# Full block masks, a softmax sink that is added on VectorE, and S5 output matrices written once to HBM and read back in long runs

## The chip, the cores and the metric

The kernel runs on one core of one Trainium2 chip, in one launch. The metric is the device time in microseconds (us). Three runs of the kernel before took 2862.04, 2859.88 and 2861.97 us; the median is 2861.97.

In the profile PE is TensorE's matmuls, PEld its weight loads, DVE VectorE, ACT ScalarE, POOL GpSimd, and SP the sync engine, which issues most DMAs. A name such as L1287 is a line of the kernel.

## The reference

Two transformer blocks over 512 positions of width 1024. The first has two layers, each with a full attention, a windowed attention with a sink, a Fourier mix, a spatial gate and a gated merge. The second has a Mamba-2 and a diff-attention layer, then one with S5 and MLA, each followed by a feed-forward network. Three places matter here. The windowed attention puts one more column, the learned sink of the head, into the softmax and drops it again:

```python
s_sink = jnp.broadcast_to(sink_f[None, :, :, None, None], s_loc.shape[:-1] + (1,))
p = jax.nn.softmax(jnp.concatenate([s_ctx, s_loc, s_sink], axis=-1), axis=-1).astype(vv.dtype)
return (jnp.einsum('bkgqn,bnkd->bqkgd', p[..., :nc], vc)
        + jnp.einsum('bkgqj,bjkd->bqkgd', p[..., nc:nc + 3 * Q_BLOCK], vv))
```

The diff attention and MLA mask their scores by chunks of 64 positions, `jax.nn.softmax(jnp.where(mask, s.astype(F32), -jnp.inf), axis=-1)`: a query sees all keys up to the end of its own chunk. In a diagonal block of 128 x 128 this masks the keys 64 to 127 for the queries 0 to 63. The S5 group is a linear state-space recurrence for 32 groups of 16 channels; the kernel works it in blocks of 8 steps, so that the output is a product of the input with shifted copies of one kernel matrix for each group, plus a product of the block's start state.

## The kernel before

Positions stand in tiles of 128 on the partitions, features in columns, or the other way round. A product in full precision is three matmuls of high and low parts (`mm3`, L237 to L239). Weights come by `wload` (L218): a 1 MB load on SP (L225) into one of two raw buffers, a cast on ScalarE (L232) and a subtraction on VectorE and GpSimd (L233). The tile framework's scheduler sets the order of instructions on each engine by dependencies and priority; only the order of the program is written out.

**Windowed attention, `attn1` (L1035).** Items are pairs of a query block and a head. `scores` multiplies queries with the high and low part of the keys (L1075, L1076), adds 128x128 block masks as a matmul with the bf16 identity as weights (L1078, `mb_id`), and writes the sink to column 768 by a matmul of one row of ones with the head's sink (L1081). There are 40 of these: 24 in layer 0 (two streams) and 16 in layer 1. A reduce takes the negated maximum (L1083), an exponential follows with a running sum (L1087). One item later come the transposes (L1097), two to three items later the values (L1111) and the division by the sum (L1122). Two score buffers in PSUM, `at`, alternate.

**Block masks of the second block, `causal64` (L1285).** The diagonal block gets its mask by a matmul with one row: weights that are 1 for the first 64 queries, times a row that is a large negative number for the last 64 keys. Diff attention calls it 64 times (tiles `dat`, after L1414 and L1415), MLA 32 times (tiles `mat`, after L2182).

**S5.** `s5_coef` (L1854) is a generator that runs beside the merge of layer 1. It works out, for four sets of 8 groups, the input matrices (`d_bm`), output matrices (`d_ca`) and kernel rows (`d_kk`, L1971) and stores each in HBM. In `odd` (L1980) the recurrence runs on VectorE in 63 steps (L2072 to L2078) beside MLA. Then comes the output. Eight DMAs read shifted windows of `d_kk` (L2237), each to 16 partitions, in pieces of 128 numbers:

```python
tt_ = self.tl(yp, [P, 32, P], F32, "s5T")
kk = self.d_kk
for k in range(8):
    nc.sync.dma_start(tt_[16 * k:16 * k + 16], kk[:, :, 16 * k:16 * k + 128])
```

For each half `pb` two loads bring `d_ca` (L2242, tiles `s5ca`), and groups of matmuls with s5T (L2250) and s5ca (L2252) follow. A few matmuls of the projection of the layer's other output (`residual`, `side`) are woven in.

Of the kernel before, what the change touches and what calls it, by code (L numbers as in the profile page):

```python
# [9 lines left out]
F32 = mybir.dt.float32  # L10
F32R = mybir.dt.float32r
BF16 = mybir.dt.bfloat16
I32 = mybir.dt.int32
AF = mybir.ActivationFunctionType
ALU = mybir.AluOpType
AX = mybir.AxisListType
PSUM = bass.MemoryType.PSUM
P = 128
# [78 lines left out]
class Kern:  # L97
# [75 lines left out]
    def setup1(self):  # L173

        nc, I = self.nc, self.I
        nc.gpsimd.dma_start(self.cst[:, P:], I["cst"][:, P:CST_KEEP])
        mk = self.mk = self.tl(self.vp, [P, 2, P], F32, "mk")
        nc.gpsimd.dma_start(mk, I["cst"][:, CST_KEEP:].rearrange("p (a b) -> p a b", a=2))
        self.sink = self.tl(self.cp, [1, 8], F32, "sink")
        nc.gpsimd.dma_start(self.sink, I["sink_d"].rearrange("a b -> (a b)").unsqueeze(0))  # L180
        for gi in (1, 2):
            self.vec_load(gi, nc.gpsimd)

    def setup_cols(self):
        for gi in (1, 2):
            self.vec_cols(gi)
        mb = self.tl(self.cp, [P, 3, P], BF16, "mb")
        self.mb_id, self.mb_prev, self.mb_next = mb[:, 0, :], mb[:, 1, :], mb[:, 2, :]
        self.G.tensor_copy(mb[:, 0, :], self.ident)
        self.G.tensor_copy(mb[:, 1:3, :], self.mk)  # L190

    def vec_load(self, gi, q):
        vr = self.vr[gi] = self.tl(self.vp, [P, P], F32, f"vr{gi}")
# [841 lines left out]
    def attn1(self, l, hds, tr, Y, full, ap, at, fills):  # L1035


        nc, V, S, G, T = self.nc, self.V, self.S, self.G, self.T
        items = [(br, i, pair, qi, j) for br in range(2) for pair in range(2) for i in ((0, 1) if full else (0,))
                 for qi in range((4, 2)[i]) for j in range(2)]  # L1040
        st = {}

        def scores(m):
            br, i, pair, qi, j = items[m]
            for f in fills:
                first, last, rate, gen, done = f
                if m >= last and (done is None or not done()):
                    for _ in gen:
                        if done is not None and done():
                            break  # L1050
                elif m >= first:
                    for _ in range(rate):
                        next(gen, None)
            tq, kh, kl = tr[br, pair]

            if i == 1:
                segs, c0 = [(512, 512, 256, ())], 512
            elif br == 0:
                segs, c0 = [(0, 0, 512, ()), (512, 512, 256, ())], 0
            else:  # L1060
                b0, b1 = max(qi - 1, 0), min(qi + 2, 4)
                nl = (b1 - b0) * P
                c0 = 512 - nl
                mk = []
                if b0 < qi:
                    mk.append((c0, self.mb_prev))
                if b1 > qi + 1:
                    mk.append((512 - P, self.mb_next))
                segs = [(c0, b0 * P, nl, mk), (512, 512, 256, ())]
            c1 = 768 + (1 if br == 1 else 0)  # L1070
            kts = [(pc + u * P, kc // P + u) for pc, kc, w, _ in segs for u in range(w // P)]
            sc = self.tl(at, [P, 1024], F32, "at")
            q0 = qi * P + (512 if i == 1 else 0)
            for pc, kc, w, mk in segs:
                T.matmul(sc[:, pc:pc + w], tq[j][:, q0:q0 + P], kh[:, kc:kc + w], start=True, stop=False)  # L1075
                T.matmul(sc[:, pc:pc + w], tq[j][:, q0:q0 + P], kl[:, kc:kc + w], start=False, stop=not mk)  # L1076
                for x, (mc, mask) in enumerate(mk):
                    T.matmul(sc[:, mc:mc + P], self.mb_id, mask, start=False, stop=x == len(mk) - 1)  # L1078
            if br == 1:
                h = l * 4 + 2 * pair + j  # L1080
                T.matmul(sc[:, 768:769], self.ones[0:1, :], self.sink[0:1, h:h + 1], start=True, stop=True)  # L1081
            mx = self.tl(self.sm, [P, 1], F32, "mx", bufs=8)
            V.tensor_reduce(mx, sc[:, c0:c1], AX.X, ALU.max, negate=True)  # L1083
            e = self.tl(ap, [P, 772], F32, "e", bufs=3)
            if qi + j == 0:
                st["sum"] = self.tl(self.sm, [P, 4, 2], F32, "sme", bufs=3)
            S.activation(e[:, c0:c1], sc[:, c0:c1], AF.Exp, bias=mx, accum_out=st["sum"][:, qi, j:j + 1])  # L1087
            st[m] = (e, kts, st["sum"])

        def transposes(m):  # L1090
            e, kts, sums = st[m]
            pt = self.tl(ap, [P, 6, P], F32, "pt", bufs=4)
            for g0 in range(0, len(kts), 4):
                grp = kts[g0:g0 + 4]
                tp = self.tl(self.tp, [P, 512], F32, "tp")
                for x, (pc, _) in enumerate(grp):
                    T.transpose(tp[:, x * P:(x + 1) * P], e[:, pc:pc + P], self.ident)  # L1097
                n = len(grp)
                (V.tensor_copy if g0 else S.copy)(pt[:, g0:g0 + n, :].rearrange("p a b -> p (a b)"), tp[:, :n * P])
            st[m] = (pt, kts, sums)  # L1100

        def values(m):
            br, i, pair, qi, _ = items[m]
            if qi == 0:
                st["po"] = self.mt()
            po = st["po"]
            _, kts, sums = st[m]
            v = hds[br][2]
            for x, (_, kt) in enumerate(kts):
                for j in range(2):  # L1110
                    T.matmul(po[64 * j:64 * j + 64, qi * P:(qi + 1) * P], v[:, kt, pair * 64:pair * 64 + 64],  # L1111
                             st[m - 1 + j][0][:, x, :], start=(x == 0), stop=(x == len(kts) - 1))
            nq = (4, 2)[i]
            if qi == nq - 1:
                self.normalised(Y(br, pair)[i][0], po, sums, nq, ap, "pt", 4)

        self.pipeline(len(items), ((scores, 0, 1), (transposes, 2, 1), (values, 3, 2)))
# [36 lines left out]
class Kern2(Kern):  # L1154
# [129 lines left out]

    def causal64(self, sc, qi):  # L1285

        self.T.matmul(sc[:, qi * P:(qi + 1) * P], self.mrow[0:1, 0, :], self.mrow[0:1, 1, :], start=False, stop=True)  # L1287

    def setup2_load(self):
        V = self.V  # L1290
        self.mrow = self.tl(self.cp, [1, 2, P], BF16, "mrow")
        V.memset(self.mrow, 0.0)
        V.memset(self.mrow[:, 0, 0:64], 1.0)
        V.memset(self.mrow[:, 1, 64:128], NEG)
        self.pos = self.tl(self.cp, [P, 4], I32, "pos")
        self.nc.gpsimd.dma_start(self.pos, self.I["positions_2"][0].rearrange("(t p) -> p t", p=P))

# [526 lines left out]
class Kern3(Kern2):  # L1824
# [22 lines left out]
    def s5_alloc(self):  # L1847
        dp = self.ctx.enter_context(self.tc.tile_pool(name="s5d", bufs=1, space=bass.MemoryType.DRAM))
        self.d_bm = [self.tl(dp, [P, 4, 2, P], F32, f"dbm{b}") for b in range(4)]
        self.d_ca = [self.tl(dp, [P, 2, 8, 64], F32, f"dca{b}") for b in range(4)]  # L1850
        self.d_kk = self.tl(dp, [16, 32, 15 * 16], F32, "dkk")
        self.a8 = self.tl(self.cp, [P, 2, 2, 16], F32, "a8")

    def s5_coef(self, pool):  # L1854
# [55 lines left out]
        for ub in range(4):  # L1910
# [61 lines left out]
            if ub == 0:  # L1972
                zt = self.tl(pool, [16, 112], F32, "s5z")
                V.memset(zt, 0.0)
                for b in range(4):
                    nc.sync.dma_start(self.d_kk[:, 8 * b:8 * b + 8, 0:112], zt.unsqueeze(1).to_broadcast([16, 8, 112]))
            yield


    def odd(self):  # L1980
# [250 lines left out]

        ys = ExitStack()
        yp = self.pool(ys, "s5y")
        tt_ = self.tl(yp, [P, 32, P], F32, "s5T")
        kk = self.d_kk
        for k in range(8):
            nc.sync.dma_start(tt_[16 * k:16 * k + 16], kk[:, :, 16 * k:16 * k + 128])  # L2237
        Y = self.tl(yp, [P, 2, 8, 8, 16], F32, "s5Y")
        for pb in range(2):
            ca = [self.tl(yp, [P, 2, 8, 4, 16], F32, f"s5ca{g2}") for g2 in range(2)]  # L2240
            for g2 in range(2):
                nc.sync.dma_start(ca[g2].rearrange("p r k u h -> p r k (u h)"), self.d_ca[2 * g2 + pb])  # L2242
            pss = [self.mt() for _ in range(2)]
            for u in range(4):
                for ri in range(3):
                    for o, g2 in ((0, 0), (1, 1), (0, 1), (1, 0)):
                        g = g2 * 16 + o * 8 + pb * 4 + u
                        dst = pss[o][64 * g2:64 * g2 + 64, u * P:(u + 1) * P]
                        if ri == 0:
                            T.matmul(dst, U[:, g, :], tt_[:, g, :], start=True, stop=False)  # L2250
                        else:
                            T.matmul(dst, xp3[64 * o:64 * o + 64, ri - 1, g2 * 8 + pb * 4 + u, :],  # L2252
                                     ca[g2][64 * o:64 * o + 64, ri - 1, :, u, :], start=False, stop=(ri == 2))
# [93 lines left out]
```

## Time and profile before

| what | value |
| --- | --- |
| median of three runs | 2861.97 us |
| the profiled execution's own time | 2858.03 us |
| its span | 2856.1 us |
| mean granted TensorE clock | 0.987 |
| TensorE busy | 2758.6 us, 97% |
| TensorE weight loads | 2287.8 us, 80% |
| VectorE busy | 1418.5 us, 50% |
| ScalarE busy | 1000.1 us, 35% |
| GpSimd busy | 897.6 us, 31% |
| HBM read, written | 231.54 MB, 6.78 MB |

The span runs from the first to the last instruction; the execution's own time is a little longer. Busy times of matmuls overlap, since they are pipelined: a record's duration is longer than the distance to the next start, and so the price of a matmul is read from starts. A weight load can lie beside the matmul before it.

### The profile page before, as it was taken

The page shows a single profiled execution, that of the slowest core. Times are in us where ns is not written, and L with a number is a line of the kernel's source. Part 1 is how long each engine was busy: PE and PEld are TensorE (multiplying, and loading weights), DVE is VectorE, ACT ScalarE, POOL GpSimd, SP SyncE. Part 2 cuts the span into 40 slices and gives each one's busy share as a digit, 9 for nine tenths or more (in the row PEclk, how much of TensorE's full clock was granted, in tenths as well). Part 3 has the DMA queues.
Part 4 walks back from the last instruction along what each step waited for, and adds up shares of the span by engine and source line. Part 5 has one row for each costly group of instructions (what it writes and reads, how often), then busy time and mean ns, then how long its engine had stood idle before and what let it go on. Part 6 is the DMA issues. An engine that isn't in the chain of part 4 may idle for free.

```text
span 2856.1 us, 39868 instructions
## 1 busy us (share of the span) xinstructions
PE 2758.6 (97%) x15976; PEld 2287.8 (80%) x15976; DVE 1418.5 (50%) x2786; ACT 1000.1 (35%) x1796; POOL 897.6 (31%) x684
## 2 busy tenths in 40 slices
PE   7999999999998999999999989999999997999998
PEld 4976888888897888888887767788888865788887
DVE  5634411113255556344667786655532384665532
ACT  3335422222343542333455333323322252432222
POOL 4400343232233134334221233533323220343332
PEclk9999999999999999999999999999999998999999
DMA  7235122121322114332322221222323204233232
GB/s 243 66 101 184 58 63 74 56 60 63 104 76 79 42 46 133 110 106 78 97 64 78 53 89 45 74 89 89 103 96 96 85 31 82 82 103 103 89 100 85
DMA packets 221165, 248.23 MB, mean 87 GB/s; under 512 B 14191, under 2 KB 205268, under 8 KB 219956
## 3 DMA queue, kind: packets, MB, share of 16 engines
q1 hardware_dynamic: 218788, 240.76, 27.3%
q0 software_dynamic: 2192, 4.93, 0.9%
q8 instruction: 125, 2.05, 0.3%
q14 instruction: 60, 0.49, 0.1%
HBM read 231.54 MB, written 6.78 MB: 83 GB/s over the span
## 4 chain that ended last, share of the span: by engine, by line
PE 42%; DVE 4%; issue 4%; DMA 2%; ACT 1%; POOL 1%; SPq 0%; ACTq 0%; POOLq 0%; DVEq 0%
PE ex L238 7%; PE ex L237 7%; PE ex L239 7%; PE mm L237 5%; PE mm L238 5%; PE mm L239 5%; DVE xs L1516 1%; PE mat L2182 1%; DMA dk<-dk 1%; PE sg L1680 1%; DMA s5T<-dkk 1%; DVE wlo L233 0%; PE mpo L2212 0%; DMA dcol<-in_ev_d_skip 0%; PE tp L2199 0%
## 5 line engine op out<-in xcount | busy, mean ns | idle before, releaser
L233 POOL TENSOR_TENSOR wlo<-wraw,whi 128x1024 fp32r<-128x1024 f32 (+3 forms) x180 | 440.4, 2447 | 888.4 <-ACT whi L232 882.2
L232 ACT CAST whi<-wraw 128x1024 fp32r<-128x1024 f32 (+2 forms) x360 | 351.6, 1006 | 600.1 <-issue 208.8
L233 DVE TENSOR_TENSOR wlo<-wraw,whi 128x1024 fp32r<-128x1024 f32 (+2 forms) x180 | 238.3, 1324 | 383.1 <-ACT whi L232 382.5
L239 PE MATMUL ex<-hhi,wlo 128*128 128x512 f32 x1044 | 408.5, 391 | 7.0 <-DVE wlo L233 7.0
L237 PE MATMUL ex<-hhi,whi 128*128 128x512 f32 x1044 | 410.0, 393 | 0.6 <-ACT whi L232 0.6
L238 PE MATMUL ex<-hlo,whi 128*128 128x512 f32 x1044 | 408.0, 391 | 0.0
L237 PE MATMUL mm<-hhi,whi 128*128 128x512 f32 x708 | 282.2, 399 | 2.4 <-ACT whi L232 2.3
L238 PE MATMUL mm<-hlo,whi 128*128 128x512 f32 x708 | 279.1, 394 | 3.1 <-DVE hlo L329 2.8
L239 PE MATMUL mm<-hhi,wlo 128*128 128x512 f32 x708 | 279.0, 394 | 2.6 <-DVE wlo L233 2.5
L239 PEld LDWEIGHTS ex<-hhi,wlo 128*128 128x128 f32 x1044 | 196.5, 188 | 50.0 <-DVE wlo L233 8.6
L237 PEld LDWEIGHTS ex<-hhi,whi 128*128 128x128 f32 x1044 | 196.6, 188 | 41.8 <-ACT whi L232 1.4
L238 PEld LDWEIGHTS ex<-hlo,whi 128*128 128x128 f32 x1044 | 196.7, 188 | 39.7
L237 PEld LDWEIGHTS mm<-hhi,whi 128*128 128x128 f32 x708 | 133.9, 189 | 32.9 <-issue 3.6
L239 PEld LDWEIGHTS mm<-hhi,wlo 128*128 128x128 f32 x708 | 133.7, 189 | 32.2 <-DVE wlo L233 3.7
L238 PEld LDWEIGHTS mm<-hlo,whi 128*128 128x128 f32 x708 | 134.0, 189 | 31.1 <-DVE hlo L329 4.1
L237 PE MATMUL mm<-whi,hhi 128*128 128x256 f32 (+1 forms) x464 | 135.3, 292 | 0.4 <-ACT hhi L257 0.4
L239 PE MATMUL mm<-whi,hlo 128*128 128x256 f32 (+1 forms) x464 | 132.5, 286 | 1.4 <-DVE hlo L329 1.4
L238 PE MATMUL mm<-wlo,hhi 128*128 128x256 f32 (+1 forms) x464 | 132.5, 286 | 0.6 <-DVE wlo L233 0.6
L237 PE MATMUL ex<-fhi,whi 128*128 128x512 f32 (+1 forms) x308 | 111.9, 363 | 0.0
L239 PE MATMUL ex<-fhi,wlo 128*128 128x512 f32 (+1 forms) x308 | 111.6, 362 | 0.0
L238 PE MATMUL ex<-flo,whi 128*128 128x512 f32 (+1 forms) x308 | 111.5, 362 | 0.0
L233 POOL TENSOR_TENSOR wblo<-wbraw,wbhi 128x256 fp32r<-128x256 f32 x32 | 27.2, 850 | 238.4 <-ACT wbhi L232 228.5
(821 smaller groups left out, 6039.9 us busy)
## 6 DMA issues: line engine op xcount, KB each, us to landing
wraw<-in_w_merge SPq DMA_DIRECT2D x32, 1024.0 KB
wraw<-in_ev_w_in SPq DMA_DIRECT2D x22, 1024.0 KB
wraw<-in_ffn_gate SPq DMA_DIRECT2D x22, 1024.0 KB
wraw<-in_ffn_up SPq DMA_DIRECT2D x22, 1024.0 KB
wraw<-in_w_in SPq DMA_DIRECT2D x20, 1024.0 KB
wraw<-in_ffn_down SPq DMA_DIRECT2D x17, 1024.0 KB
wraw<-in_w_ada SPq DMA_DIRECT2D x16, 1024.0 KB
wbraw<-in_w_br SPq DMA_DIRECT2D x32, 256.0 KB
```

The costliest lines, as they stand in the source:

```text
L232: self.S.copy(hi[:, a:b], raw[:, a:b])
L233: e.tensor_tensor(lo[:, a:b], raw[:, a:b], hi[:, a:b].bitcast(F32), ALU.subtract)
L237: self.T.matmul(ps, lh, rh, start=first, stop=False)
L238: self.T.matmul(ps, lh, rl, start=False, stop=False)
L239: self.T.matmul(ps, ll, rh, start=False, stop=last)
L1516: V.scalar_tensor_tensor(o, cv[:, tap:tap + 512], cw[:, tap * 12 + t:tap * 12 + t + 1], o, ALU.mult, ALU.add)
L1680: T.matmul(sg[:, j * P:(j + 1) * P], mk, self.c("uincl"), start=True, stop=True)
L2182: T.matmul(sc[:, :n], qT[:, qi * P:(qi + 1) * P], kT[:, :n], start=True, stop=False)
```

## The change

There are three parts. The sink is loaded to all partitions and kept twice, as it is and negated; its matmul goes, a VectorE minimum after the reduce brings it into the negated maximum, and once for a group of query blocks `sinks` adds exp(sink - maximum) to the sums. The mask of `causal64` is a full 128 x 128 bf16 matrix, multiplied by the identity. And at the end of `s5_coef` 16 DMAs copy the shifted windows of `d_kk`, HBM to HBM, to `d_tt`, in two halves, each laid out as the tile in which it is read; `odd` then loads each half with one DMA of 8 KB for each partition, the second behind the first half's `s5ca`.

```diff
-        self.sink = self.tl(self.cp, [1, 8], F32, "sink")
-        nc.gpsimd.dma_start(self.sink, I["sink_d"].rearrange("a b -> (a b)").unsqueeze(0))
+        self.sink = self.tl(self.cp, [P, 2, 8], F32, "sink")
+        nc.gpsimd.dma_start(self.sink[:, 0, :], I["sink_d"].rearrange("a b -> (a b)").unsqueeze(0).to_broadcast([P, 8]))
...
+        self.G.tensor_scalar(self.sink[:, 1, :], self.sink[:, 0, :], -1.0, None, ALU.mult)
...
-            c1 = 768 + (1 if br == 1 else 0)
+            c1 = 768
...
+            if qi + j == 0:
+                st["sum"] = self.tl(self.sm, [P, 4, 2], F32, "sme", bufs=3)
+                st["mx"] = self.tl(self.sm, [P, 4, 2], F32, "smx", bufs=3)
+            mx = st["mx"][:, qi, j:j + 1]
+            V.tensor_reduce(mx, sc[:, c0:c1], AX.X, ALU.max, negate=True)
             if br == 1:
                 h = l * 4 + 2 * pair + j
-                T.matmul(sc[:, 768:769], self.ones[0:1, :], self.sink[0:1, h:h + 1], start=True, stop=True)
-            mx = self.tl(self.sm, [P, 1], F32, "mx", bufs=8)
-            V.tensor_reduce(mx, sc[:, c0:c1], AX.X, ALU.max, negate=True)
-            e = self.tl(ap, [P, 772], F32, "e", bufs=3)
-            if qi + j == 0:
-                st["sum"] = self.tl(self.sm, [P, 4, 2], F32, "sme", bufs=3)
+                V.tensor_tensor(mx, mx, self.sink[:, 1, h:h + 1], ALU.min)
+            e = self.tl(ap, [P, 768], F32, "e", bufs=3)
...
+        def sinks(m):
+
+            br, i, pair, qi, j = items[m]
+            nq = (4, 2)[i]
+            if br == 0 or qi + j < nq:
+                return
+            h, mx, sums = l * 4 + 2 * pair, st["mx", m], st[m][2]
+            V.tensor_tensor(mx[:, :nq], mx[:, :nq], self.sink[:, 0, h:h + 2].unsqueeze(1).to_broadcast([P, nq, 2]), ALU.add)
+            S.activation(mx[:, :nq], mx[:, :nq], AF.Exp)
+            V.tensor_tensor(sums[:, :nq], sums[:, :nq], mx[:, :nq], ALU.add)
...
-        self.T.matmul(sc[:, qi * P:(qi + 1) * P], self.mrow[0:1, 0, :], self.mrow[0:1, 1, :], start=False, stop=True)
+        self.T.matmul(sc[:, qi * P:(qi + 1) * P], self.mb_id, self.mrow, start=False, stop=True)
...
-        self.mrow = self.tl(self.cp, [1, 2, P], BF16, "mrow")
+        self.mrow = self.tl(self.cp, [P, P], BF16, "mrow")
         V.memset(self.mrow, 0.0)
-        V.memset(self.mrow[:, 0, 0:64], 1.0)
-        V.memset(self.mrow[:, 1, 64:128], NEG)
+        V.memset(self.mrow[0:64, 64:128], NEG)
...
+        self.d_tt = [self.tl(dp, [P, 4, 4, P], F32, f"dtt{b}") for b in range(2)]
...
+        for pb in range(2):
+            for k in range(8):
+                nc.sync.dma_start(self.d_tt[pb][16 * k:16 * k + 16],
+                                  self.d_kk.rearrange("h (a b u) n -> h a b u n", b=2, u=4)[:, :, pb, :, 16 * k:16 * k + 128])
+            yield
...
-        tt_ = self.tl(yp, [P, 32, P], F32, "s5T")
-        kk = self.d_kk
-        for k in range(8):
-            nc.sync.dma_start(tt_[16 * k:16 * k + 16], kk[:, :, 16 * k:16 * k + 128])
+        tt_ = [self.tl(yp, [P, 4, 4, P], F32, f"s5T{pb}") for pb in range(2)]
+        nc.sync.dma_start(tt_[0], self.d_tt[0])
...
+            if pb == 0:
+                nc.sync.dma_start(tt_[1], self.d_tt[1])
...
-                            T.matmul(dst, U[:, g, :], tt_[:, g, :], start=True, stop=False)
+                            T.matmul(dst, U[:, g, :], tt_[pb][:, g2 * 2 + o, u, :], start=True, stop=False)
```

The instructions of TensorE in the windowed branch of layer 0, before; `at` are score tiles, `tp` transposes:

```order
L1075 MATMUL at_2939<-tk_2305,tq_2374 128x256
L1076 MATMUL at_2939<-tk_2305,tq_2374 128x256
L1081 MATMUL at_2939<-sink_146,ones_77 128x1
L1097 MATMUL tp_2930<-cst_76,e_2851 128x128 x4
L1097 MATMUL tp_2936<-cst_76,e_2851 128x128
```

and after, where L1076, L1077 and L1112 are the lines that were L1075, L1076 and L1097:

```order
L1076 MATMUL at_2914<-tk_2297,tq_2364 128x256
L1077 MATMUL at_2914<-tk_2297,tq_2364 128x256
L1112 MATMUL tp_2905<-cst_76,e_2828 128x128 x4
L1112 MATMUL tp_2911<-cst_76,e_2828 128x128
L1126 MATMUL mm_2802<-pt_2874,hkv_171 64x128
```

The row with the sink is gone, and the transposes stand right behind the scores.

SP's transfers at the end of the merge of layer 1, before; `wraw` and `wbraw` are weight loads, `dca`, `dbm` and `dkk` the S5 stores:

```order
L225 DMA wraw_11587<-in_w_merge 128x8x256
L1941 DMA dca_17_113<-s5ca_11331 256x1x512
L225 DMA wbraw_11579<-in_w_br 128x2x256
L225 DMA wraw_11718<-in_w_merge 128x8x256
L225 DMA wbraw_11710<-in_w_br 128x2x256
L225 DMA wraw_11812<-in_w_out 128x8x256
L1957 DMA dbm_13_109<-s5bm_11529 128x1024
L1971 DMA dkk_114<-s5kk_11595 16x128 x8
L225 DMA wraw_11884<-in_w_out 128x8x256
```

and after, where `dtt_19` and `dtt_20` are the halves of the new copy:

```order
L226 DMA wraw_11539<-in_w_merge 128x8x256
L1996 DMA dtt_19_115<-dkk_114 256x1x128
L1956 DMA dca_17_113<-s5ca_11283 256x1x512
L1996 DMA dtt_19_115<-dkk_114 256x1x128
L226 DMA wbraw_11531<-in_w_br 128x2x256
L1996 DMA dtt_19_115<-dkk_114 256x1x128 x6
L1972 DMA dbm_13_109<-s5bm_11481 128x1024
L226 DMA wbraw_11670<-in_w_br 128x2x256
L226 DMA wraw_11678<-in_w_merge 128x8x256
L226 DMA wraw_11780<-in_w_out 128x8x256
L1986 DMA dkk_114<-s5kk_11547 16x128 x8
L226 DMA wraw_11852<-in_w_out 128x8x256
```

The first half's copies stand ahead of the last store of `dbm`, and this now ahead of the last load of `w_merge`; the second half's copies stand between loads of `w_out`.

SP's transfers at the S5 output, before; `s5T` and `s5ca` are the matrices that the output matmuls read:

```order
L225 DMA wraw_21554<-in_od_w_out 128x4x256
L2237 DMA s5T_21310<-dkk_114 16x32x128 x8
L2242 DMA s5ca_3671_21320<-dca_14_110 128x1024
L2242 DMA s5ca_3672_21321<-dca_16_112 128x1024
L225 DMA wraw_21576<-in_od_w_glu 128x4x512
L2242 DMA s5ca_3676_21377<-dca_17_113 128x1024
L2242 DMA s5ca_3675_21376<-dca_15_111 128x1024
```

and after:

```order
L226 DMA wraw_21517<-in_od_w_out 128x4x256
L2256 DMA s5T_3603_21278<-dtt_19_115 128x2048
L2261 DMA s5ca_3606_21282<-dca_14_110 128x1024
L2261 DMA s5ca_3607_21283<-dca_16_112 128x1024
L2263 DMA s5T_3604_21279<-dtt_20_116 128x2048
L226 DMA wraw_21539<-in_od_w_glu 128x4x512
L2261 DMA s5ca_3611_21340<-dca_17_113 128x1024
L2261 DMA s5ca_3610_21339<-dca_15_111 128x1024
```

Eight transfers have become one before the `s5ca` loads and one behind them; the next weights follow in both.

## Rows read from the trace of the kernel before

**Rows 1.** Profile page, part 1: engine, busy time, share of the span, instructions.
```profile
PE 2758.6 (97%) x15976; PEld 2287.8 (80%) x15976; DVE 1418.5 (50%) x2786; ACT 1000.1 (35%) x1796; POOL 897.6 (31%) x684
```

**Rows 2.** Windows: stretch, length, busy PE, PEld, DVE, ACT, POOL, clock, DMA share, GB/s.
```profile
1030.00:1260.00 230.00, 230.00 (x1069) 187.57 (x1068) 119.75 (x270) 72.33 (x121) 98.34 (x73) 1.00 0.37 112
1345.00:1600.00 255.00, 247.08 (x1766) 219.43 (x1765) 173.77 (x391) 120.63 (x283) 65.21 (x42) 0.99 0.29 75
2290.00:2380.00 90.00, 83.70 (x546) 57.13 (x546) 81.66 (x374) 46.27 (x120) 17.20 (x21) 0.96 0.08 25
```

**Rows 3.** Timeline of TensorE at the S5 output: start, duration, instruction, idle before.
```profile
2403.16 1.30 PE L2250 MATMUL ex<-s5T,U 128*64 128x128 f32 x9 [14.07 <-DMA s5T<-dkk]
```

**Rows 4.** Instructions of line 1081, the sink: count, duration min/median/max.
```profile
L1081 PE MATMUL at<-sink,ones x80: 245/256/267, 257.1 to 1019.4; 1*128 1x1 f32 x80
```

**Rows 5.** Timeline of TensorE in the windowed branch of layer 0.
```profile
256.48 0.28 PE L1076 MATMUL at<-tk,tq 128*128 128x256 f32 x1
256.60 0.23 PE L1078 MATMUL at<-mb 128*128 128x128 bf16 x1
256.64 0.36 PE L1075 MATMUL at<-tk,tq 128*128 128x256 f32 x1
256.84 0.28 PE L1076 MATMUL at<-tk,tq 128*128 128x256 f32 x1
257.05 0.38 PE L1081 MATMUL at<-sink,ones 1*128 1x1 f32 x2
257.36 0.44 PE L1097 MATMUL tp<-cst,e 128*128 128x128 f32 x2
```

**Rows 6.** Instructions of line 1122, reciprocals of softmax sums.
```profile
L1122 DVE RECIPROCAL rsm<-sme x16: 178/194/204, 212.1 to 2377.4; 128x8 f32<-128x8 f32 x12, 128x4 f32<-128x4 f32 x4
```

**Rows 7.** Who waited for the exponential of line 1087: total us, times.
```profile
  PEld at L1075: 3.9, 4
```

**Rows 8.** Instructions of line 1287, the row mask: its weight loads.
```profile
L1287 PEld LDWEIGHTS <-mrow x96: 90/90/98, 1365.7 to 2375.4; 1*128 1x128 bf16 x96
```

**Rows 9.** Timeline of TensorE in diff attention, around one row mask.
```profile
1387.91 0.40 PE L1415 MATMUL dat<-dk,dtq 128*128 128x512 f32 x1
1388.24 0.23 PE L1287 MATMUL dat<-mrow 1*128 1x128 bf16 x1
1388.39 0.50 PE L1414 MATMUL dat<-dk,dtq 128*128 128x512 f32 x1
```

**Rows 10.** Instructions of line 1078, the 128-row mask of the windowed branch: weight loads.
```profile
L1078 PEld LDWEIGHTS <-mb x48: 95/96/101, 256.6 to 1018.8; 128*128 128x128 bf16 x48
```

**Rows 11.** Timeline of TensorE in MLA, a row mask and what follows.
```profile
2327.05 0.22 PE L1287 MATMUL mat<-mrow 1*128 1x128 bf16 x1
2327.21 0.55 PE L2199 MATMUL tp<-cst,hhi 128*128 128x128 f32 x3
```

**Rows 12.** Timeline of SP, the sync queue, at the S5 output.
```profile
2380.36 9.86 SPq L2237 DMA_DIRECT2D s5T<-dkk  x8
```

**Rows 13.** Chain of waits from 2380 to 2420 us: start, duration, what.
```profile
2387.85 15.17 DMA s5T<-dkk
...
2412.94 3.69 DMA s5ca<-dca
```

**Rows 14.** Windows: the 8 us after the S5 wait, columns as in rows 2.
```profile
2403.00:2411.00 8.00, 7.84 (x66) 5.28 (x66) 0.00 (x0) 0.00 (x0) 0.00 (x0) 0.50 0.56 216
```

**Rows 15.** Timeline of SP in the merge of layer 1.
```profile
1211.59 0.39 SPq L225 DMA_DIRECT2D wraw<-in_w_merge  x1
...
1242.80 0.34 SPq L1957 DMA_DIRECT2D dbm<-s5bm  x1
```

**Rows 16.** Profile page, part 5: the GpSimd half of a weight split.
```profile
L233 POOL TENSOR_TENSOR wlo<-wraw,whi 128x1024 fp32r<-128x1024 f32 (+3 forms) x180 | 440.4, 2447 | 888.4 <-ACT whi L232 882.2
```

**Rows 17.** Timeline of TensorE in the merge of layer 1.
```profile
1248.89 1.14 PE L1964 MATMUL tp<-s5ca,s5bp 128*64 128x128 f32 x16
```

More of the change, by code (lines that the diff above doesn't have):

```diff
@@ L1078, in scores @@
                     T.matmul(sc[:, mc:mc + P], self.mb_id, mask, start=False, stop=x == len(mk) - 1)
+            if qi + j == 0:
[3 more added lines that the diff above has]
+            V.tensor_reduce(mx, sc[:, c0:c1], AX.X, ALU.max, negate=True)
             if br == 1:
                 h = l * 4 + 2 * pair + j
-                T.matmul(sc[:, 768:769], self.ones[0:1, :], self.sink[0:1, h:h + 1], start=True, stop=True)
-            mx = self.tl(self.sm, [P, 1], F32, "mx", bufs=8)
-            V.tensor_reduce(mx, sc[:, c0:c1], AX.X, ALU.max, negate=True)
-            e = self.tl(ap, [P, 772], F32, "e", bufs=3)
-            if qi + j == 0:
-                st["sum"] = self.tl(self.sm, [P, 4, 2], F32, "sme", bufs=3)
+                V.tensor_tensor(mx, mx, self.sink[:, 1, h:h + 1], ALU.min)
+            e = self.tl(ap, [P, 768], F32, "e", bufs=3)
             S.activation(e[:, c0:c1], sc[:, c0:c1], AF.Exp, bias=mx, accum_out=st["sum"][:, qi, j:j + 1])
             st[m] = (e, kts, st["sum"])
+            st["mx", m] = st["mx"]
+        def sinks(m):
[7 more added lines that the diff above has]
+            V.tensor_tensor(sums[:, :nq], sums[:, :nq], mx[:, :nq], ALU.add)
         def transposes(m):
+            sinks(m)
             e, kts, sums = st[m]
```

## Prediction

> **What bounds the kernel now.** I read first the page's line of engine times: TensorE is busy 2758.6 us, 97% of the span [rows 1]. What it no longer has to do, or no longer stands behind, shortens the run one for one wherever nothing else ends later. So the second view was the windows over the four stages that the change touches [rows 2]. From 1030 to 1260 us (the layer-1 merge, in whose shadow the S5 coefficients are made) TensorE is busy 230.00 of 230 us: a copy there costs nothing unless it holds up a weight load. From 1345 to 1600 us (diff attention) TensorE is busy 247.08 of 255 and VectorE 173.77: TensorE is the bound, though not at every moment. From 2290 to 2380 us (MLA and the S5 recurrence) VectorE is busy 81.66 of 90 and TensorE 83.70: two bounds side by side. The third view was the TensorE timeline around single masks and sink matmuls, the fourth the waits and the sync queue (SP) at the S5 output, where one wait of 14.07 us stands [rows 3].
>
> **The sink (40 items).** The line of the sink has 80 matmul records, two for each of 40 matmuls [rows 4]. In the timeline L1076 starts at 256.84, the sink at 257.05, the next transpose at 257.36: 0.52 us from the last score matmul to what follows it. The same score matmul before a full 128-row mask takes 0.12 us, and the mask's own follower starts 0.04 later (L1076 at 256.48, mask at 256.60, next matmul at 256.64) [rows 5]. So up to 0.40 us goes per item, 40 x 0.40 = 16. Where a values matmul with 64-column weights follows instead of a transpose, part of the gap should stay, since it changes the shape of the array too; I take 40 x 0.31 = 12.4, and keep 0 and 16 as ends. Added are 40 VectorE minima of 128x1 and, for 6 groups (two pairs, two streams in layer 0 and one in layer 1), two VectorE additions and one small exponential. The nearest row for such an instruction is the reciprocal on 128x8, 194 ns [rows 6]: 40 x 0.19 + 12 x 0.19 = 10 us of VectorE, and about 1.2 us of ScalarE at the same price. They lie beside TensorE, whose work runs one to three items behind the scores: in the whole of this attention TensorE's weight loads for new scores waited for an exponential 4 times, 3.9 us in all [rows 7]. The minimum stands between reduce and exponential; queued behind it on VectorE are copies and the next reduce. If that cover were gone, each item would be late by its 0.19 us and a hand-off, together 12 us at 0.3 each: that is the lower end, 12 us lost instead of 12.4 won. The sums get their sink just before the group's transposes, with three items until they are used. The sink column also leaves reduce and exponential (513 to 512 columns), which is nothing.
>
> **The diff masks (64).** Of the 96 row masks [rows 8], 64 stand here: 8 heads, 4 query blocks, 2 parts. L1415 (512 columns) starts at 1387.91, the mask at 1388.24, the next score at 1388.39: 0.33 and 0.15 us, 0.48 together [rows 9]. A 512-column matmul of the merge takes 230 us / 1069, about 0.215 us, on average [rows 2], and the full mask of the windowed branch lets its follower start 0.04 us later [rows 5]: 0.26 together. Saved 0.22 each, 64 x 0.22 = 14.1 us. The trace does show the 128-row bf16 mask, though only beside 256-column scores, and so the price is a transfer. TensorE was idle 7.9 us in this stage [rows 2]; some of those waits will be longer once it arrives sooner. I take 12.5 us, with 0 and 14.1 as ends.
>
> [...] The mask's weight load took 90 ns with one row [rows 8] and 96 ns with 128 rows [rows 10]. [...] But the starts of [rows 9] show that the cost isn't in the load: the matmul before the mask is followed 0.33 us later, that behind it 0.15 us later, as if nothing were loaded ahead around a one-row matmul. [...]
>
> **The MLA masks (32, the rest of 96).** Here the scores have 96 rows. The mask starts at 2327.05 and the transpose at 2327.21, 0.16 us [rows 11] instead of 0.04 [rows 5]; with something saved ahead of it I take 0.15 x 32 = 4.8 us. As VectorE is as good as full in this stage [rows 2], half is kept: 2.4 (ends 0 and 5).
>
> **The S5 matrices.** Before, eight transfers of 16x32x128 (runs of 512 bytes) are issued from 2380.36 on, 9.86 us of issuing [rows 12], and the last lands 15.17 us after 2387.85, at 2403.02 [rows 13]: 22.7 us for 2 MB. [...] Long runs have their row in the same stage: the two s5ca loads of 512 KB each (4 KB per partition) land 3.69 us after issue, 1 MB [rows 13]. After, SP issues s5T[0] (1 MB), two s5ca, s5T[1], the next weights: by that rate they land at about 2384.1, 2387.7, 2391.4 and 2395.1. TensorE comes at 2403.16 - 14.07 = 2389.1, so the first two have arrived. The first half's matmuls took 9.8 us, mostly at half clock, so about 5: at 2394 the second s5ca pair can start, behind the weights, and lands at about 2398.8; TensorE has 12 matmuls to put in (2.6 us) and waits some 2.2. With 0.3 for the rest of the first load, new waits are 2.5. Term: 14.1 + 4 - 2.5 = 15.6 us. Ends: 0, if the load is no faster, and 18, if nothing is waited for.
>
> [...]
>
> **The copies (16).** They are 131 KB each in 512-byte runs, DRAM to DRAM, which no row shows. Behind the merge weight load of 1211.59 the first eight now stand, and then the store dbm, issued at 1242.80 [rows 15]; the next merge load moves behind both, to about 1243.5, and later if the copies block the queue. It then needs 3.7 us to land, and its split ends with a GpSimd subtraction of 2.4 [rows 16]; with as much again for the casts ahead of that, an estimate, it is usable at 1252.1. TensorE first needs it after the block of L1964 that starts at 1248.89 and lasts 1.14 [rows 17] and some 60 matmuls of 0.215: 1262.9. That is 10.8 us of slack, so I cost the move at 0. The second eight stand behind the last small stores of the coefficients and ahead of loads for the output projection; the first of these was issued well before, and TensorE has its matmuls to go through. The copies would have to hold SP for longer than 31 us from 1211.6 to reach even dbm; at the price of the s5T issues eight hold it for 10 [rows 12].
>
> **Sum.** 12.4 + 12.5 + 2.4 + 15.6 = 42.9. The profiled execution took 2858.03 us, so 2815.1; it was 3.9 us under the median 2861.97. On the scale of the median: 2819 us.
>
> **Rivals.**
> (a) Everything is kept: 16 + 14.1 + 5 + 18 = 53, 2809 us. For it speaks TensorE's 97%; against it the waits that already stand in the stages.
> (b) Full masks cost what row masks cost: 14.9 less, 2834. For it the equal load times [rows 8, 10], against it the starts [rows 9].
> (c) The S5 load is no faster: 15.6 less, 2835. [...]
> (d) The chain scores, reduce, minimum, exponential becomes the bound in the windowed branch: 12 lost instead of 12.4 won, 2843. Against it the four waits of [rows 7].
> (e) The other side: the copies block SP in the merge. From 1211.6 on, the load behind them is issued at 1211.6 + 8c, where c is what one copy holds the queue, and is usable 8.6 us later. What lies beyond 1262.9 is lost, and it eats the whole 43 us when c is over 10.7 us. At c = 12 the wait is 53.3 and the run takes 2872. Against it: eight s5T issues held the queue 9.86 us altogether, 1.2 each [rows 12].
> That the change doesn't do what it says isn't a rival: in the order of instructions the sink matmuls are gone and the load stands in two pieces.
>
> **Chances.** The forecast (2811 to 2827) 0.58; (a) 0.12; (b) 0.09; (c) 0.06; (d) 0.08; (e) 0.03; two of (b) to (d) together, which comes to the old time within a few us, 0.04. A measurement here tells 0.2%, 5.7 us, from no change. Faster then has 0.93, same 0.04, slower 0.03. The likeliest case's own range is 2811 to 2827; the 8-in-10 range reaches from all of (a), 2804, to (b) and (c) with a little room, 2838.
>
> **What would show it.** Right: the wait of L2250 (now another line) for s5T gone or under 3 us and the clock near 1 there; the start from last score to transpose in the windowed branch 0.12 us; the follower of a mask 0.04 us behind it; no TensorE wait from 1030 to 1260 us. Wrong: new waits for exponentials in the windowed branch (d), mask gaps of 0.33 and 0.15 still there (b), s5T landing 20 us after issue (c), or weight waits in the merge (e).

## The result, and the profile after

The changed kernel takes 2812.22 us at the median of four runs (2810.49 to 2816.7), against 2862.01 for the kernel before: a ratio of 0.9827 with an interval of 0.981 to 0.9844, 49.8 us less. The forecast was 2819, in a range from 2804 to 2838. The profiled execution took 2810.49 us, its span 2808.7.

Where the time went can be read by laying the two traces side by side: how much earlier does the same instruction of TensorE start?

| from, to (us in the trace before) | what lies there | gained there |
| --- | --- | --- |
| 0 to 250 | start | -0.7 |
| 250 to 400 | windowed branch, layer 0 (24 sinks) | 8.6 |
| 800 to 806 | start of layer 1 | -1.6 |
| 970 to 1030 | windowed branch, layer 1 (16 sinks) | 6.0 |
| 1030 to 1345 | merge of layer 1, start of the second block | 0.7 |
| 1345 to 1600 | diff attention (64 masks) | 9.7 |
| 2290 to 2380 | MLA (32 masks) | 5.4 |
| 2380 to 2420 | S5 output | 19.1 |

The rows add to 47.2 us; the two profiled executions differ by 47.5, the medians by 49.8. The lines below follow [rows 1 to 17]. First the page's engine times and the windows over the same stages, the columns as in [rows 2] (the third begins 4.6 us early, as it has the length of the one before):

```profile
PE 2716.6 (97%) x15896; PEld 2269.8 (81%) x15896; DVE 1423.4 (51%) x2837; ACT 1000.8 (36%) x1802; POOL 895.9 (32%) x685
```

```profile
1018.00:1248.00 230.00, 230.00 (x1071) 188.13 (x1070) 119.48 (x270) 72.58 (x121) 98.38 (x73) 1.00 0.39 115
1331.90:1577.00 245.10, 233.44 (x1765) 215.63 (x1764) 173.46 (x391) 119.75 (x283) 65.32 (x42) 0.99 0.31 78
2262.00:2352.00 90.00, 82.76 (x611) 61.30 (x611) 83.25 (x390) 47.81 (x122) 17.37 (x21) 0.96 0.08 25
```

TensorE lost 42 us of busy time and kept its 97%. The merge is still without a gap: 230.00 of 230. In diff attention TensorE is now idle 11.7 us of 245 where it was 7.9 of 255. No kernel that was tried is faster than the changed one by more than the intervals.

Then the TensorE timeline of the windowed branch (start, duration), which answers to [rows 5], and of diff attention, which answers to [rows 9]:

```profile
257.31 0.23 PE L1079 MATMUL at<-mb 128*128 128x128 bf16 x1
257.35 0.36 PE L1076 MATMUL at<-tk,tq 128*128 128x256 f32 x1
257.55 0.28 PE L1077 MATMUL at<-tk,tq 128*128 128x256 f32 x1
257.67 0.38 PE L1112 MATMUL tp<-cst,e 128*128 128x128 f32 x2
...
1373.59 0.40 PE L1429 MATMUL dat<-dk,dtq 128*128 128x512 f32 x1
1373.83 0.23 PE L1302 MATMUL dat<-mrow,mb 128*128 128x128 bf16 x1
1373.87 0.48 PE L1428 MATMUL dat<-dk,dtq 128*128 128x512 f32 x1
```

The transpose follows the last score matmul 0.12 us later, not 0.52. Around the mask 0.33 and 0.15 us have become 0.24 and 0.04, though the mask's weight load takes 95 to 96 ns where the row's took 90 [rows 8]. Next what TensorE waited for in diff attention, after and (second block) before: total us, times, longest.

```profile
PE tp L1458 <- DVE dk L259: 6.3, 3, 2.1
PE dat L1428 <- DMA dk<-dk: 1.8, 2, 1.4
```

```profile
PE tp L1444 <- DVE dk L258: 4.3, 3, 1.5
...
PE dat L1414 <- DMA dk<-dk: 0.6, 1, 0.6
```

Here 3.2 us were given back: the first two waits grew from 4.9 to 8.1. Last the S5 output: SP's issues, TensorE's first matmuls (answering to [rows 3, 12]), the window over the first half of its work (answering to [rows 14]), and the SP queue in the merge (answering to [rows 15]).

```profile
2351.61 0.34 SPq L2256 DMA_DIRECT2D s5T<-dtt  x1
2352.00 0.91 SPq L2261 DMA_DIRECT2D s5ca<-dca  x2
2352.95 0.61 SPq L2263 DMA_DIRECT2D s5T<-dtt  x1
```

```profile
2359.88 0.39 PE L240 MATMUL ex<-hhi,wlo 128*128 128x512 f32 x1
2360.20 0.66 PE L2271 MATMUL ex<-s5T,U 128*64 128x128 f32 x8
2360.79 0.67 PE L2273 MATMUL ex<-s5ca,xp 64*64 64x128 f32 x16
```

```profile
2360.00:2366.00 6.00, 6.00 (x108) 4.21 (x107) 1.02 (x2) 0.89 (x2) 0.00 (x0) 1.00 0.67 221
```

```profile
1211.20 3.80 SPq L1996 DMA_DIRECT2D dtt<-dkk  x6
1229.93 0.35 SPq L1972 DMA_DIRECT2D dbm<-s5bm  x1
...
1230.82 0.76 SPq L226 DMA_DIRECT2D wraw<-in_w_merge  x1
```

TensorE comes to its first S5 matmul without a wait, at a granted clock of 1.00 where it was 0.50. In the merge six copies hold SP for 3.80 us; the last load of w_merge goes out at 1230.82, directly behind dbm.

### The profile page after: what moved, and what is told of

It reads as the page before. It is cut to its first block, busy times and chain, and to the rows that moved or that the text cites. A ratio compares the mean times of both kernels' runs of the same rounds, so it can differ in the third digit from the quotient of the medians.

```text
span 2808.7 us, 39749 instructions
## 1 busy us (share of the span) xinstructions
PE 2716.6 (97%) x15896; PEld 2269.8 (81%) x15896; DVE 1423.4 (51%) x2837; ACT 1000.8 (36%) x1802; POOL 895.9 (32%) x685
```

## The experiments

Each kernel changes the one before or the changed one. Times are medians, ratios are to the kernel before, with their interval; the edits are cut to their core.

**One part at a time.** The first three are the kernel before with the sink's hunks of the diff, with those of `causal64` and `mrow`, and with those of `d_tt` and s5T.

> The sink's part alone, the rest as before. Theory A (the parts are separate pieces of TensorE's path and add up): 0.52 us from score matmul to transpose becomes 0.12, 40 x 0.40 = 16 us won, less about 1 us at the start where the broadcast sink load stands ahead of others: 2846 to 2849 us, no new wait for an exponential. Theory B (the parts share cover, so one alone gives less): under 10 us won, 2853 or more, with TensorE waits for exponentials of 5 us or more in the windowed branch.

> The full 128-row masks of the second block alone. Theory A: diff attention gives about 10 us and MLA about 5, as the two traces show when they are laid side by side: 2845 to 2849 us. Theory B (the S5 load starts when MLA ends but TensorE waits for it anyway, so MLA's part is worth something only together with the S5 part): 10 us, 2851 to 2853. By equal weight loads (90 and 96 ns): no change, 2860 to 2864.

> The copies and the long reads alone. Theory A: the wait of 14.07 us goes and the half clock behind it (8 us at 0.50, so 4 us) with it, new waits 0 to 1: 17 to 19.5 us won, 2842 to 2845. Theory B (the clock falls elsewhere in that stage instead): 14 us won, 2847 to 2849. In both no TensorE wait in the merge of layer 1.

Measured: sink 2845.29 us (0.9949, 0.9934 to 0.9964), masks 2842.09 (0.9935, 0.9922 to 0.9948), S5 2844.68 (0.9948, 0.9936 to 0.9961). The three shortfalls add to 1.68%, the whole change has 1.73%: within the intervals the parts are separate, as theory A has it. The stages say the same: alone, the sink gains 14.6 us in its two branches, the masks 9.2 in diff attention and 5.9 in MLA, S5 19.0 at its output. The sink's time lies 0.7 us below its expected range, that of the masks 3 below. The masks didn't need the S5 part: TensorE's wait for s5T stayed at 14.1 us and came earlier (the surplus of 3 us lies at the S5 output). S5 alone came out near the weak end: other stages lose 9 us in that execution, most of it in spells at half clock that the kernel before didn't have, or had shorter. One that it didn't have (stretch, busy times, then the clock 0.53, where the kernel before has 1.00 from 1327 to 1334 us):

```profile
1331.00:1338.00 7.00, 7.00 (x37) 7.00 (x36) 2.01 (x13) 1.38 (x3) 0.00 (x0) 0.53 0.44 148
```

Such spells differ from trace to trace, in stages that nobody edited; of differences of 2 to 5 us I therefore read the stage and not the total.

**What makes a one-row matmul dear.** In the kernel before, the sink from a matmul over all rows:

```diff
-                T.matmul(sc[:, 768:769], self.ones[0:1, :], self.sink[0:1, h:h + 1], start=True, stop=True)
+                T.matmul(sc[:, 768:769], self.ident, self.sink[:, h:h + 1], start=True, stop=True)
```

> The kernel before, but the sink column comes from a matmul with all 128 rows (identity weights times the sink in every partition) and not from one row of ones. It tells the one row from the matmul itself. Theory A (the gaps come from the change between a full array and one row): the sink costs 2 records of about 0.06 us and small gaps, some 0.1 to 0.15 us instead of 0.40, 10 to 12 us won, 2850 to 2852. Theory C (a matmul of its own with a new weight load costs it, whatever its rows): 0 to 3 us won, 2859 to 2862.

2851.39 us (0.9969, 0.9957 to 0.9981). The same matmul, with all rows:

```profile
261.17 0.28 PE L1076 MATMUL at<-tk,tq 128*128 128x256 f32 x1
261.29 0.28 PE L1081 MATMUL at<-sink,cst 128*128 128x1 f32 x2
261.43 0.41 PE L1097 MATMUL tp<-cst,e 128*128 128x128 f32 x2
```

From last score matmul to transpose 0.26 us, against 0.52 with one row and 0.12 without the matmul. So 0.26 of the 0.40 belonged to the one row, and 0.14 to the matmul. Then, in the changed kernel, masks of 64 rows:

```diff
-        self.T.matmul(sc[:, qi * P:(qi + 1) * P], self.mb_id, self.mrow, start=False, stop=True)
+        self.T.matmul(sc[:, qi * P:(qi + 1) * P], self.mb_id[0:64, :], self.mrow[0:64, :], start=False, stop=True)
```

> The changed kernel, but the 96 masks of the second block use only the first 64 rows of identity and mask (the others are zero, the result is the same). It tells what makes the one-row mask dear. Theory A (a matmul on part of the array's rows behind one on all rows, or the reverse, is not overlapped): gaps of 0.15 us behind the mask and 0.09 us before it come back, about 10 us lost in diff attention and up to 5 in MLA against the changed kernel: 2822 to 2828 us. Theory C (only one row is dear, or the load's own form): the starts stay at 0.04 us and the time at 2809 to 2816.

2828.17 us (0.9882, 0.9868 to 0.9896), 16 more than the changed kernel and all that the masks had won:

```profile
1351.69 0.28 PE L1429 MATMUL dat<-dk,dtq 128*128 128x128 f32 x1
1351.89 0.23 PE L1302 MATMUL dat<-mrow,mb 64*128 64x128 bf16 x1
1352.05 0.39 PE L239 MATMUL mm<-wlo,hhi 128*128 128x256 f32 x1
```

0.20 and 0.16 us: these are the gaps of one row, which behind the same 128-column record has 0.21 and 0.155 in the trace of the kernel before (full masks: 0.12 and 0.04). And in the changed kernel, MLA's scores with 128 rows, not 96 (tiles of 128 rows, the last 32 set to zero on GpSimd):

```diff
-            t = self.tl(ap, [96, 512], F32, "mqT", bufs=4)
-            (S.copy if h < 2 else V.tensor_copy)(t, ps[0:96])
+            t = self.tl(ap, [P, 512], F32, "mqT", bufs=4)
+            (S.copy if h < 2 else V.tensor_copy)(t[0:96], ps[0:96])
+            G.memset(t[96:P], 0.0)
```

> The changed kernel with the queries and keys of MLA padded from 96 to 128 rows with zeros (16 small GpSimd memsets), so that its score matmuls fill the array's rows as their neighbours do. In the trace of the changed kernel the second of two score records of 96 rows stands about 0.15 us later than its columns need, 32 times, and about 0.1 more lies at 21 changes to the mask. Theory A (part of the rows is what costs): 5 to 8 us won in MLA, 2804 to 2808. Rival (VectorE is the bound there by now): 0 to 3 us, 2809 to 2814.

2813.36 us (0.9828, 0.9815 to 0.9842): nothing won. The time is the rival's, but not for its reason, VectorE: no gap closed at all. Changed kernel, then this one:

```profile
2320.13 0.39 PE L2203 MATMUL mat<-mkT,mqT 96*128 96x128 f32 x2
2320.36 0.22 PE L1302 MATMUL mat<-mrow,mb 128*128 128x128 bf16 x1
2320.41 0.61 PE L2220 MATMUL tp<-cst,hhi 128*128 128x128 f32 x4
```

```profile
2322.97 0.39 PE L2205 MATMUL mat<-mkT,mqT 128*128 128x128 f32 x2
2323.20 0.22 PE L1302 MATMUL mat<-mrow,mb 128*128 128x128 bf16 x1
2323.25 0.61 PE L2222 MATMUL tp<-cst,hhi 128*128 128x128 f32 x4
```

96 rows cost what 128 cost (0.23 us for the two records, 0.05 from mask to transpose in both). So 1 and 64 rows are dear here between matmuls of 128 (0.21 and 0.155 us before and behind a mask of one row, 0.20 and 0.16 with 64, against 0.12 and 0.04 with 128), and 96 are not. What makes them dear the three runs don't show.

**The chain of the windowed branch.** Changed kernel, `for _ in range(4):` around the minimum.

> The changed kernel with the VectorE minimum done four times per item (the result is the same): 120 more instructions of about 0.1 us each in the chain from scores to exponential. Theory A (the chain is covered by work that runs one to three items behind): within 3 us of the changed kernel, 2809 to 2816. Rival (d) of the prediction (the chain is as good as the bound there): 0.3 us for each of 40 items and more, 12 us or more lost, 2824 or more.

2818.84 us (0.9848, 0.9835 to 0.9861), 6.6 more than the changed kernel, though the two intervals touch; its trace loses 5.5 in the branch of layer 0 (up to 1.7 of them at half clock) and 2.2 in layer 1. TensorE's waits for exponentials there between 240 and 370 us, with four minima and with one:

```profile
PE at L1076 <- ACT e L1090: 4.4, 5, 2.1
```

```profile
PE at L1076 <- ACT e L1089: 1.7, 3, 0.7
```

So the cover is thin: neither theory's number was met, and rival (d) is half right. Three more minima are not hidden, and the first isn't quite: the sink's part alone shows the same 1.7 us, and like the changed kernel 0.6 more in layer 1, where the kernel before and the one with the full sink matmul show no such wait. Whether the minimum makes these 2.3 us, or TensorE's earlier arrival, is not told apart.

**The copies' price.** Changed kernel, each copy written four times.

> The changed kernel with every copy of the shifted matrices written four times (three of them to places that nobody reads): 64 DMAs instead of 16 on SP in the merge of layer 1. It looks for the point from which rival (e) decides. Theory A (a copy holds the queue 0.65 us, as in the changed kernel, where six took 3.80 and eight 5.34): 32 take 21 us, the last load of w_merge moves by less than its slack, no wait in the merge, 2809 to 2816. Rival (e) (the queue fills and each copy holds it for as long as its packets run): some us for each, the load 30 us or more late, a wait of 10 to 40 us in the merge: 2822 to 2855.

2837.01 us (0.9912, 0.9898 to 0.9925), 25 more, all in the merge. SP's last load of w_merge there:

```profile
1256.20 0.47 SPq L226 DMA_DIRECT2D wraw<-in_w_merge  x1
```

TensorE's one line of waits from 1020 to 1340 us, and the window behind the late load (columns as in [rows 2]):

```profile
PE ex L238 <- ACT whi L233: 21.9, 2, 15.0
```

```profile
1256.00:1290.00 34.00, 18.02 (x63) 13.46 (x64) 6.93 (x9) 7.26 (x10) 3.83 (x3) 0.70 0.86 231
```

The last w_merge load goes out at 1256.20 in place of 1230.82. Each copy holds SP for about 0.65 us, as theory A said, but the load now stands behind the last dkk stores as well, and TensorE waits 21.9 us for splits and gets 0.70 of its clock. Rival (e) is a real mechanism at four times the dose. Only the first of the two waits is for this load, the other is for one of w_out. It shows the slack at the actual dose, here the wait and, from the changed kernel, the cast (split) of the same load:

```profile
1265.00 0.80 PE L238 MATMUL ex<-hhi,whi 128*128 128x512 f32 x1 [15.03 <-ACT whi L233]
...
1240.13 2.00 ACT L233 CAST whi<-wraw 128x1024 fp32r<-128x1024 f32 x2 [2.55 <-DMA wraw<-in_w_merge]
1250.86 0.39 PE L238 MATMUL ex<-hhi,whi 128*128 128x512 f32 x1
```

With four copies the cast starts at 1263.90, and TensorE goes on 1.1 us later. In the changed kernel it starts at 1240.13 and TensorE needs it at 1250.86, so that 9.6 us of slack are left; the prediction had 10.8.

**What made the s5T load slow.** Four kernels. The first stores the copies so that one wide DMA reads pieces of 512 bytes; the second leaves 64 bytes free behind every 512 in the s5T tiles:

```diff
-        self.d_tt = [self.tl(dp, [P, 4, 4, P], F32, f"dtt{b}") for b in range(2)]
+        self.d_tt = [self.tl(dp, [4, 4, P, P], F32, f"dtt{b}").rearrange("a u p n -> p a u n") for b in range(2)]
...
-        tt_ = [self.tl(yp, [P, 4, 4, P], F32, f"s5T{pb}") for pb in range(2)]
+        tt_ = [self.tl(yp, [P, 4, 4, 144], F32, f"s5T{pb}")[:, :, :, 0:P] for pb in range(2)]
```

> The changed kernel, but the copies lie in HBM in such an order that each half of s5T is read by one DMA in 512-byte runs and not in runs of 8 KB. It tells the run length from the number and spread of the DMAs. Theory A (512-byte runs are slow, 2 MB took 22.7 us): a half takes about 11 us to land, so TensorE waits some 4 to 8 us for it or for the s5ca loads behind it: 2817 to 2824 us. Theory D (512 bytes run at full rate, and it was eight issues to 16 partitions each that were slow): each half lands in about 4 us, no wait, 2809 to 2816.

> The changed kernel with a gap of 64 bytes behind every 512 bytes of the s5T tiles, so that one DMA over 128 partitions must write single pieces of 512 bytes. Theory E (narrowness was slow): each half lands in about 4 us, no wait, 2809 to 2816. Theory F (single 512-byte packets are slow, 89 ns each where they were slow before): 2048 packets over 16 engines, 11 us for a half, TensorE waits 4 to 10 us, 2817 to 2826.

The third reads 8 KB runs, 16 partitions to a DMA, in the changed kernel; the fourth is the kernel before with one wide DMA straight from `d_kk`:

```diff
-        nc.sync.dma_start(tt_[0], self.d_tt[0])
+        for k in range(8):
+            nc.sync.dma_start(tt_[0][16 * k:16 * k + 16], self.d_tt[0][16 * k:16 * k + 16])
...
-        for k in range(8):
-            nc.sync.dma_start(tt_[16 * k:16 * k + 16], kk[:, :, 16 * k:16 * k + 128])
+        src = bass.AP(src.tensor, src.offset, [[16 * n[0], 8], r, g, n])
+        nc.sync.dma_start(tt_, src)
```

> The changed kernel with each half of s5T read by eight DMAs of 16 partitions each, as before, but in runs of 8 KB. It tells narrow transfers from short runs, after wide reads in 512-byte pieces had cost nothing. Theory E (transfers to 16 partitions are slow, whatever their runs, and eight issues of 0.6 to 1.2 us come on top): a half takes 8 us or more to land, TensorE waits 5 us or more at the S5 output: 2817 to 2830 us. Theory F (single 512-byte packets to the chip's own memory are what is slow, not the narrow shape): the waits are only those of the issues, 0 to 4 us, 2810 to 2817.

> The kernel before with one edit: its eight s5T loads are one DMA over all 128 partitions, straight from the stored matrix, in windows of 512 bytes that overlap, with no copies. Theory E (narrow transfers were slow): 2 MB land in 7 to 9 us, TensorE waits 0 to 3 us instead of 14.07, and the time is that of the S5 part alone, 2842 to 2848. Theory F (512-byte packets or overlapping windows are slow): 2 MB take 20 us or more, 2856 to 2864.

Measured: 2812.06 us (0.9824, 0.9811 to 0.9838) and 2809.3 (0.9816, 0.9801 to 0.9831), both as fast as the changed kernel; 2822.14 (0.9857, 0.9843 to 0.987), 10 more; 2868.33 (1.0019, 1.001 to 1.0028), slower than before and above the ranges of both theories. What the DMAs moved while s5T loaded, in this order: before (2382 to 2402 us), changed (2353 to 2360), pieces of 512, padded tiles, narrow, direct:

```profile
DMA packets 4218, 2.22 MB, mean 111 GB/s; under 512 B 128, under 2 KB 4182, under 8 KB 4218
```

```profile
DMA packets 521, 2.83 MB, mean 404 GB/s; under 512 B 48, under 2 KB 48, under 8 KB 304
```

```profile
DMA packets 756, 1.92 MB, mean 296 GB/s; under 512 B 32, under 2 KB 32, under 8 KB 755
```

```profile
DMA packets 451, 2.27 MB, mean 324 GB/s; under 512 B 47, under 2 KB 47, under 8 KB 301
```

```profile
DMA packets 274, 1.13 MB, mean 141 GB/s; under 512 B 127, under 2 KB 127, under 8 KB 145
```

```profile
DMA packets 3231, 1.65 MB, mean 89 GB/s; under 512 B 0, under 2 KB 3231, under 8 KB 3231
```

And the windows over the old load and the direct one, DMA share next to last:

```profile
2382.00:2402.00 20.00, 6.74 (x29) 4.86 (x27) 7.58 (x25) 1.76 (x3) 2.58 (x2) 0.80 1.22 111
2384.50:2403.00 18.50, 7.55 (x32) 5.55 (x30) 8.38 (x29) 2.19 (x4) 2.60 (x2) 0.85 0.59 89
```

Pieces of 512 bytes in memory cost little, on either side: the trace shows them in packets of 2 KB and 8 KB, at 296 and 324 GB/s for all loads of the stretch together. Narrow loads are slow with long runs too: a packet of 8 KB takes on average some 900 ns (estimated from 129 of them in 8 us, with 16 engines at 97%) in place of 333, and 1 MB some 8 us from its first packet to its last in place of 3.3. TensorE waits 5.8 us for s5T and s5ca, and the half clock is back (0.50 from 2364.9 to 2371.7). Theory E named that rightly. But it is not all: the direct load is wide and slower still, 18.9 us of wait. It moves 512 bytes to a packet, as before, and in it the packets took 59% of the time of 16 engines at 89 GB/s, where the old load's took 122% (packets overlap). Whether its small packets made it slow or something else, this run doesn't tell. Nor does a run show why the narrow loads moved 141 GB/s where the wide one moved 404.

## Why the prediction was right, and where it wasn't

**Sum.** 42.9 us were forecast for the profiled execution; it became 47.5 shorter, and the median 49.8. The mechanism of each part was there; the sizes were off in all four terms, and one reason was wrong. That the sum came so near is in part luck: the diff masks fell short by 2.8 us where the others gave more.

**Sink, 12.4 forecast, 14.6 measured in the two branches.** The 0.12 us were met. The discount to 0.31 on all 40 was too large: only 8 sinks were followed by a values matmul with 64-column weights, and there 0.52 us became 0.21 (0.12 before a transpose); behind the others the full 0.40 went. That makes 15.3 us. New waits for exponentials (2.3 us) count against it, so that some 1.6 us were won elsewhere in the branches; where is open. The sink with all rows shows what the 0.40 is made of.

**Diff masks, 12.5 forecast, 9.7 measured.** The gap around a mask closed by 0.20 us, as worked out (0.22). But 3.2 us came back as waits for the next heads' keys (L1458 for VectorE, L1428 for a DMA). The text had named such waits and left 1.6 for them.

**MLA masks, 2.4 forecast, 5.4 measured.** The step that failed: "As VectorE is as good as full in this stage [rows 2], half is kept". The gaps around a mask closed by 0.19 us (0.21 and 0.155 us became 0.11 and 0.06), 6.1 us for 32, and 5.4 were kept. Little was lost to VectorE: TensorE's one long wait for it grew from 4.7 to 5.4 us (before and after; total, times, longest):

```profile
PE tp L2199 <- DVE s5ta L2074: 4.7, 1, 4.7
...
PE tp L2220 <- DVE s5ta L2095: 5.4, 1, 5.4
```

Busy shares of 81.66 and 83.70 of 90 said nothing about which one was waited for.

**S5, 15.6 forecast, 19.1 measured.** The wait of 14.07 us went, and the new waits are 0.2 us, not 2.5. The half clock went too. In the kernel before, eight matmuls of L2250 take 1.05 us at half clock:

```profile
2410.00 1.12 PE L2250 MATMUL ex<-s5T,U 128*64 128x128 f32 x8
2411.05 0.67 PE L2252 MATMUL ex<-s5ca,xp 64*64 64x128 f32 x16
```

After the change they take 0.59 (2360.20 to 2360.79 above). Group by group, the 7.9 us at half clock cost 3.4, near the 4 forecast, which are half of the 8 us at a granted clock of 0.50 [rows 14]. The remaining 1.5 us of the gain are mostly order: 24 matmuls of the projection stood between S5's before, 19 stand there now, and five come later.

In the load the reason was wrong. The step: "22.7 us for 2 MB" in runs of 512 bytes, against 1 MB of s5ca in 3.69 us [rows 13] ("Long runs have their row in the same stage"): three times as long per byte, read as the price of short runs. Wide loads in 512-byte pieces, on either side, lost nothing; the narrow shape ran at a third of the rate with long runs. The old load's first packets took 27 ns for 512 bytes, later ones 89, so the size alone isn't what made them slow. Still, 512 bytes in 27 ns are 19 GB/s in one packet, 8 KB in 309 ns (the median) are 26.5. The copies gained because they allow a wide load in large packets. In the narrow shape long packets raised the rate only from 111 to 141 GB/s, the wide shape then to 404: long runs alone, with the loads kept narrow, would have gained little. What 512-byte packets by themselves cost in a wide load is open: the direct load alone had them.

**The rivals.** (b) is refuted by the starts and by the masks of 64 rows, though the load times are nearly equal (90, 92 and 96 ns for 1, 64 and 128 rows); (c) by the trace; (a) came close, 3 us below the result; (d) is near, as the four minima show; (e) needs more copies than there are: the last w_merge load moved as forecast (1230.82 is 1243.6 on the scale of the kernel before, forecast 1243.5), within its slack.

## What to carry to other kernels

A small matmul on 1 or 64 rows between full ones cost 0.2 us of TensorE and more here (0.20 for a mask of 128 columns, 0.26 for the sink's one column): fill it up with zeros, or take it off the engine. A load's price is read from its partitions before its run length: here runs of 8 KB moved 404 GB/s over 128 partitions and 141 over 16 at a time, and pieces of 512 bytes over 128 partitions 296 and 324 (each time all loads of the stretch together; the direct load, wide too, moved 89, and why was not shown); if a layout forbids a wide load, a copy in memory buys one, and here 16 copies were hidden (9.6 us of slack were left). Next to such a gain look at the clock: here the wait that went took the stretch at half clock behind it along (0.50, then 1.00).

## What was not expected of the hardware

- A score matmul with 96 rows between full ones costs no gap (0.23 us for its two records, as with 128 rows), a mask matmul with 64 costs 0.08 us before and 0.12 behind it (0.20 and 0.16 us in place of 0.12 and 0.04).
- The same 512-byte packet took 27 ns in the copies and in the first microsecond of the old load, about 54 on average in the direct load and 89 in the old load under way.
- A spell of 3.4 us at half clock appeared at 793.7 us of the changed kernel, right behind a wait that the kernel before had as well (1.11 and 1.13 us): it cost 1.6 us. In the kernel before no spell stood there.
